# First MLP of a two-layer backbone: which of two engines splits the weights, and in what order output blocks are summed

## The chip, the cores and the metric

The kernel is one program on one core of a Trainium2 chip. The metric is device time in microseconds (us) of one execution. The kernel before took 1520.66 us (median of three runs, 1517.83 to 1520.87). The engines are named as the profile names them: PE is TensorE's matmuls and PEld its weight loads, DVE is VectorE, ACT ScalarE, POOL GpSimd, SP the queue of SyncE from which nearly all transfers start.

## The reference, cut to what matters

Two layers run over 512 latent tokens ("x") and a context of 256 ("c"), each of 1024 features. A layer normalises and modulates its tokens, projects them, mixes them in three parallel heads (windowed attention, gated chunks, a Fourier transform), projects back, and ends with an MLP:

```
def squared_relu_mlp(h, w1, w2):
    return jnp.square(jax.nn.relu(h @ w1)) @ w2      # w1 1024 x 4096, w2 4096 x 1024
...
    x = x + g1 * rmsnorm(y, g_post_mix[l])
    hx2 = rmsnorm(x, g_pre_ff[l]) * (1.0 + sc2) + sh2
    x = x + g2 * rmsnorm(squared_relu_mlp(hx2, w_ff1[l], w_ff2[l]), g_post_ff[l])
```

The scales and shifts come from a modulation, a product of a vector with a 1024 x 6144 weight for each layer. In the second layer the context ends after its keys and values, so its MLP has x alone; the first layer's MLP has x and c.

## The kernel before, in words

Every float32 operand of TensorE is kept as two parts, a high part (a rounded copy, made by ACT) and a low part (operand less high part), and each product is three: high by high, high by low, low by high. Making a low part is an elementwise instruction with two operands, which DVE or POOL can do.

The MLP runs over 16 groups of 256 hidden features. Groups 0 and 1 are plain products (`ff1_open`, `ff1`). From group 2 on the product with w1 is a Winograd form of Strassen's: `wino_open` loads two raw tiles of the group (L1133), makes eight weight operands "11", "21", "t1", "t2", "12", "t3", "t4", "22" (in that order) in `parts` (L1147 high part on ACT, L1148 low part) and the four differences between them in `sub` (L1152, which overwrite the raw tiles `raw_f`). `wino` then runs the products: tiles `w` and `wt` for x (L1182), `wc` for the context (L1195, `plain`). DVE adds them up (L1201, tiles `p`, `u`, `c`), and ACT makes the squared ReLU (`hidden`, L1122 to L1125) with tiles `hx` for x and `hc` for c. The features come in this order: first half of the tokens, first half of the group (`c11`); context, first half; second tokens, second half (`c22`); second tokens, first half (`c21`); first tokens, second half (the last sum, `u`, from the product `w22`); context, second half.

`ff2_open` loads two units of w2, 128 x 1024 each, and splits them (`wunit`: L234 high on ACT, L235 low, tile `lo_f`). `ff2` adds the group's products for one output block of 128 tokens (L1247, PSUM tiles `f2...`, three banks in turn) to its sum Y on DVE (L1251). In the first layer it goes over x2, x3, x0, x1, c0, c1, and after each block takes one step `ada` of the next modulation: a 512 KB load and two DVE multiply-adds of 128x1024 (L264, L266, tile `acc`).

What sets the order: each engine runs its own list in order. The program is scheduled when it is built: instructions go by the order of the code, as soon as the scheduler holds their inputs ready, and `high_priority(offset=...)` moves a part ahead by so many places; `HP` is that offset for `wino`. The table `LOADS` says, by layer, which engine takes each low part and difference: `lo1` and `diff1` begin anew with every group, `lo2` and `loh` run on through the layer. A `v` is DVE, a `p` POOL. In the first layer's mixing `MIX` says which steps of other work PE gets behind each attention unit (`flow`): `u`, `g`, `f` project one token block, `U`, `G`, `F` load their weights, `fc`, `fx` step through the Fourier part, `gc`, `gx` load a gate, `oc`, `ox` step through the output projection, `ada` through a modulation. Units are divided by `|`.

Of the kernel before, what the change touches and what calls it, by code (L numbers as in the profile page):

```python
# [18 lines left out]
P = 128  # L19
# [12 lines left out]
# How far the first product of the MLP goes ahead of other work.  # L32
HP = 5
# The engine (v or p) that takes each of the two-operand steps of a hidden group: low parts of the weights of the
# first and second product, differences of weights, low parts of the hidden features.
LOADS = {
    (0, 'lo1'): "vppvvppv",
    (0, 'diff1'): "vppv",
    (0, 'lo2'): "vp",
# [6 lines left out]
# What the tensor engine does beside the attention units of a layer: U, G, F load the weights of a column group  # L46
# of the in-projection and u, g, f project a token block with them, fc, fx step through the Fourier mixing,
# gc, gx load the gates, oc, ox step through the output projection, ada through a modulation.
MIX = (
    'U u u | u u u u G | ada ada g | ada g g ada ada g | g g ada | ada ada F f | f fc | f f f fc f fc | gc fx | gx oc fx oc oc | fx | ox ox ox ox oc',  # L50
    'U u u u G u g F g | | f f f f g | fx fx g fx | | | ox | ox ox ox gx',
# [10 lines left out]
def _bc(ap, n, axis):  # L62
    """ap with a broadcast dimension of n put in at free position `axis`."""
    v = ap.unsqueeze(axis)
    shape = list(v.shape)
    shape[axis] = n
    return v.to_broadcast(shape)
# [3 lines left out]
def kernel(ctx: ExitStack, tc: tile.TileContext, a: dict, out: bass.AP):  # L71
    nc = tc.nc
    PSUM = bass.MemoryType.PSUM
# [13 lines left out]
    # Temporaries of a chain come from h1, h2, h3 in this order, so that chains never wait in a circle.  # L87
# [9 lines left out]
    # Streams that run side by side have tiles of their own; within a tag tiles are handed out in program order.  # L97
# [25 lines left out]
    F = bank("F", 3)  # L123
# [9 lines left out]
    # ------------------------------------------------------------- constants  # L133
# [18 lines left out]
    def rows_in(name, width, pairs):  # L152
        """Rows at given partitions of a zeroed [32, width] tile."""
# [6 lines left out]
    def turned(t, name, use):  # L160
        """Feature-major pieces of four chunks of such rows in PSUM, handed to `use`."""
# [7 lines left out]
    # silu(c), silu(c_ctx) as two columns of a zero-padded stationary operand  # L169
# [18 lines left out]
    ones = unit[:, 1:2]  # L188
# [18 lines left out]
    # ---------------------------------------------------- common small helpers  # L207
# [4 lines left out]
    def power(o, i, scale, bias, expo):  # L212
        """o = (i * scale + bias) ** expo"""
# [11 lines left out]
    def wunit(src, shape, name, lo_eng=None, part=None, hi_pool=False):  # L225
        """A weight unit in two float32r parts whose sum is the float32 weight."""
# [11 lines left out]
    # ------------------------------------------------------------------ adaLN  # L238
    # modc[l]: feature-major columns for (sh1, sc1, sh2, sc2); gates go to DRAM rows.
# [7 lines left out]
    def ada_quad(l, q, alloc, alloct, wtile, side=None):  # L247
        """A sixth of the modulation of a layer. side: the rows of the weight times their entries are summed over
        the row chunks beside the tensor engine, which is left with the sum over the partitions."""
# [73 lines left out]
    def ada_rest(steps, alloc, alloct, side=None):  # L323
        """Steps through (layer, quad), one row chunk of the weight at a time."""
        for l, q in steps:
            yield from ada_quad(l, q, alloc, alloct, wa, side)
# [6 lines left out]
    # ------------------------------------------------- feature-major activations  # L333
    class Feat:
        """Feature-major tokens in two float32r parts, eight chunks of 128 features: with a tile for
        every chunk (whole=True, wide moving operands) or tiles for every token block."""
# [1077 lines left out]
```

## Time and profile before

| | us |
|---|---|
| median of three timed runs | 1520.66 (1517.83 to 1520.87) |
| span of the profiled execution | 1516.8 |
| PE busy | 1429.4 (94%) |
| DVE busy | 1115.8 (74%) |
| ACT busy | 747.7 (49%) |
| POOL busy | 644.3 (42%) |

Of the profiled execution the page gives the span, from its first to its last instruction; the median of the timed runs lies 3.9 us above it. Busy shares are means over unlike stages: the start (to about 106 us), mixing of the first layer (to 341), its MLP (to about 923), mixing of the second layer (to about 1140), its MLP. The page's list of costliest groups has both engines' instructions of the lines that the change touches, each with its idle time before it and what ended that idle time; a time in the queries counts from the span's start.

### The profile page before, as it was taken

The numbers are of one execution on the slowest core, as the hardware profiler recorded it, in microseconds if no ns is written. First come the engines' busy times: TensorE is split into PE (matmuls) and PEld (weight loads), VectorE is DVE, ScalarE is ACT, GpSimd is POOL, SyncE is SP. The second block draws the span as 40 slices with busy tenths as digits, with TensorE's granted clock in tenths as the row PEclk, the third lists the DMA queues.
The fourth block names the chain that finished last, engine by engine and source line by source line (L and its number), as shares of the span: only waits on it lengthen the run. The fifth ranks groups of instructions, "written<-read, shape, count | busy, mean of one in ns | idle before, by whom it ended". The sixth has DMA issues, their size and how long they took to land. (4 is left out here: it accounts for less than half of the span.)

```text
span 1516.8 us, 24509 instructions
## 1 busy us (share of the span) xinstructions
PE 1429.4 (94%) x9133; PEld 1252.7 (83%) x9133; DVE 1115.8 (74%) x2003; ACT 747.7 (49%) x1673; POOL 644.3 (42%) x608
## 2 busy tenths in 40 slices
PE   7999999999899999999989998999998899999997
PEld 4688798788788878888878887998777788989886
DVE  3366887858687877878777758788757987777685
ACT  3346666556534333343333445476656555554452
POOL 3212636646634333334433546234346644344241
PEclk9999999999999999999999999999998999999999
DMA  9634322435132332325554344213134133223322
GB/s 328 228 122 154 112 74 84 137 115 167 42 100 84 124 111 84 126 70 174 167 172 129 125 160 139 72 55 87 39 100 165 56 112 111 93 89 100 110 84 84
DMA packets 94352, 177.58 MB, mean 117 GB/s; under 512 B 5796, under 2 KB 59524, under 8 KB 94232
## 3 DMA queue, kind: packets, MB, share of 16 engines
q1 hardware_dynamic: 91224, 170.93, 35.0%
q0 software_dynamic: 3008, 5.08, 1.2%
q8 instruction: 72, 1.18, 0.3%
q14 instruction: 48, 0.39, 0.1%
HBM read 166.62 MB, written 9.46 MB: 116 GB/s over the span
## 5 line engine op out<-in xcount | busy, mean ns | idle before, releaser
L1152 POOL TENSOR_TENSOR raw_f<-raw_f,raw_f 128x512 f32<-128x512 f32 x70 | 98.2, 1402 | 107.8 <-DVE raw_f L1152 89.5
L1147 ACT CAST Wf<-raw_f 128x512 fp32r<-128x512 f32 x98 | 60.4, 619 | 118.6 <-DMA raw_f<-in_w_ff 108.4
L266 DVE SCALAR_TENSOR_TENSOR acc<-wa,silu,acc 128x1024 f32<-128x1024 f32 x70 | 96.1, 1391 | 21.7 <-DMA wa<-in_w_ada 21.6
L1148 POOL TENSOR_TENSOR Wf<-raw_f,Wf 128x512 fp32r<-128x512 f32 x28 | 40.1, 1433 | 153.3 <-ACT Wf L1147 153.3
L1195 PE MATMUL wc<-f01c,Wf 128*128 128x256 f32 x672 | 98.5, 286 | 3.4 <-DVE p L1201 3.4
L1195 PEld LDWEIGHTS wc<-f01c,Wf 128*128 128x128 f32 x672 | 91.6, 194 | 7.9 <-DVE p L1201 3.8
L1148 DVE TENSOR_TENSOR Wf<-raw_f,Wf 128x512 fp32r<-128x512 f32 x70 | 62.0, 887 | 41.0 <-ACT Wf L1147 40.9
L234 ACT CAST hi_f<-raw_f 128x1024 fp32r<-128x1024 f32 x72 | 73.8, 1043 | 34.8 <-PE f208c L1247 6.6
L235 POOL TENSOR_TENSOR lo_f<-raw_f,hi_f 128x1024 fp32r<-128x1024 f32 x20 | 54.7, 2735 | 77.7 <-ACT hi_f L234 57.6
L1125 DVE TENSOR_TENSOR hx<-r,hx 128x256 fp32r<-128x256 f32 x98 | 61.5, 630 | 31.2 <-ACT r L1124 31.1
L235 DVE TENSOR_TENSOR lo_f<-raw_f,hi_f 128x1024 fp32r<-128x1024 f32 x52 | 76.6, 1478 | 1.3 <-ACT hi_f L234 1.0
L1123 ACT ACTIVATE hx<-r 128x256 fp32r<-128x256 f32 x112 | 45.4, 413 | 44.4 <-PE f203x L1247 8.7
L1182 PE MATMUL w<-f11x,Wf 128*128 128x256 f32 x336 | 65.1, 283 | 0.0
L1182 PE MATMUL w<-S,Wf 128*128 128x256 f32 x336 | 63.0, 283 | 0.0
L1122 ACT ACTIVATE r<-c 128x256 f32<-128x256 f32 x84 | 34.7, 414 | 55.5 <-DVE c L1201 43.4
L1182 PEld LDWEIGHTS w<-f11x,Wf 128*128 128x128 f32 x336 | 54.7, 191 | 1.5
L1182 PEld LDWEIGHTS w<-S,Wf 128*128 128x128 f32 x336 | 53.0, 191 | 1.7 <-issue 0.4
L1182 PE MATMUL w<-f01x,Wf 128*128 128x256 f32 x336 | 50.4, 284 | 1.9 <-ACT Wf L1147 1.0
L1182 PEld LDWEIGHTS w<-f01x,Wf 128*128 128x128 f32 x336 | 46.4, 191 | 5.3 <-ACT Wf L1147 1.4
L1124 ACT ACTIVATE r<-r 128x256 f32<-128x256 f32 x112 | 45.5, 413 | 1.9
L393 ACT ACTIVATE xvx<-xTx,mod 128x256 f32<-128x256 f32 x64 | 31.6, 560 | 18.2 <-PE xTx L379 11.9
L797 ACT ACTIVATE E0x<-E0x,mx_0x 128x512 f32<-128x512 f32 (+1 forms) x32 | 24.9, 778 | 12.9 <-DVE mx_0x L791 12.7
(1243 smaller groups left out, 4886.1 us busy)
## 6 DMA issues: line engine op xcount, KB each, us to landing
raw_f<-in_w_ff SPq DMA_DIRECT2D x128, 512.0 KB
wa<-in_w_ada SPq DMA_DIRECT2D x80, 512.0 KB
wq<-in_w_ada SPq DMA_DIRECT2D x16, 512.0 KB
raw_out0c<-in_w_out SPq DMA_DIRECT2D x8, 512.0 KB
raw_out0x<-in_w_out SPq DMA_DIRECT2D x8, 512.0 KB
res0x<-xr0x SPq DMA_DIRECT2D x8, 512.0 KB
raw_out1x<-in_w_out SPq DMA_DIRECT2D x8, 512.0 KB
xl0x<-in_x SPq DMA_DIRECT2D x4, 512.0 KB
```

Of the source, the lines that this page charges most:

```text
L234: nc.scalar.copy(hi, raw)
L235: (lo_eng or nc.vector).tensor_tensor(out=lo, in0=raw, in1=hi.bitcast(F32), op=ALU.subtract)
L266: nc.vector.scalar_tensor_tensor(out=acc[r], in0=w, scalar=s, in1=acc[r], op0=ALU.mult, op1=ALU.add)
L1122: nc.scalar.activation(r, src, AF.Relu)
L1123: nc.scalar.activation(hv[:, 0], r, AF.Square)
L1124: nc.scalar.activation(r, r, AF.Square)
L1125: next(lo_h).tensor_tensor(out=hv[:, 1], in0=r, in1=hv[:, 0].bitcast(F32), op=ALU.subtract)
L1147: nc.scalar.copy(t[:, 0], src)
L1148: next(lo).tensor_tensor(out=t[:, 1], in0=src, in1=t[:, 0].bitcast(F32), op=ALU.subtract)
L1152: next(diff).tensor_tensor(out=o, in0=x, in1=y, op=ALU.subtract)
L1182: nc.tensor.matmul(ps, W[w][:, wl, k], A[k // 2][:, k % 2, xh], start=(m == 0), stop=(m == 11))
L1195: nc.tensor.matmul(ps, W[f"{k // 4 + 1}{j + 1}"][:, wl, k % 4], f2["c"].ap(k, xh, 0, CTX), start=(m == 0), stop=(m == 3 * KD - 1))
```

## The change

In the table of the first layer, `lo1` gives POOL three of eight low parts and not four ("21" goes to DVE), `diff1` one of four differences and not two (the one kept in tile b21, `raw_f`'s second), and `lo2` none of the low parts of w2 where it had every second one. Of a pattern of 16 letters for `lo1` only the first eight are used, since it begins anew with each group. The order of output blocks becomes x1, x2, x0, x3, c0, c1 in the first layer and x3, x0, x1, x2 in the second. `HP` goes from 5 to 4. In both layers some steps of the mixing move by a unit. Comment lines are gone as well.

```
-HP = 5
+HP = 4
 LOADS = {
-    (0, 'lo1'): "vppvvppv",
-    (0, 'diff1'): "vppv",
-    (0, 'lo2'): "vp",
+    (0, 'lo1'): "vvpvvppvvvpvvppv",
+    (0, 'diff1'): "vpvv",
+    (0, 'lo2'): "vv",
     (0, 'loh'): "vpvpvv",
...
 MIX = (
-    'U u u | u u u u G | ada ada g | ada g g ada ada g | g g ada | ada ada F f | f fc | f f f fc f fc | gc fx | gx oc fx oc oc | fx | ox ox ox ox oc',
-    'U u u u G u g F g | | f f f f g | fx fx g fx | | | ox | ox ox ox gx',
+    'U u u | u u u u G | ada ada g | ada g g ada ada ada g | g | ada g ada F f | f fc | f f f fc f fc | fx gc | gx oc fx oc oc | fx | ox ox ox ox oc',
+    'U u u u G u g F g | f | f f g | f fx fx g fx |  |  | ox | ox ox ox gx',
 )
...
+        order = ((("x", 1), ("x", 2), ("x", 0), ("x", 3), ("c", 0), ("c", 1)),
+                 (("x", 3), ("x", 0), ("x", 1), ("x", 2)))[l]
         for g in range(2, NG):
...
-                for kd, b in [(kd, b) for kd, b in (("x", 2), ("x", 3), ("x", 0), ("x", 1), ("c", 0), ("c", 1)) if kd in kinds]:
+                for kd, b in order:
                     ff2([g], kd, b)
                     next(ada, None)
```

In the order below, names carry layer, group and part: `Wf106t3` is operand t3 of layer 0, group 6, `raw_f1060` the first raw tile of w1 of that group, `lo_f2061` the low part of its second unit of w2, `hx060` and `hx061` the first and second half of its features. POOL's list for group 6 of the first layer, before:

```order
L1148 TENSOR_TENSOR Wf10621_6229<-raw_f1061_6221,Wf10621_6229 128x512
L1148 TENSOR_TENSOR Wf106t1_6233<-raw_f1060_6219,Wf106t1_6233 128x512
L1152 TENSOR_TENSOR raw_f1060_6219<-raw_f1061_6221,raw_f1060_6219 128x4x128
L1152 TENSOR_TENSOR raw_f1061_6221<-raw_f1061_6221,raw_f1060_6219 128x4x128
L1125 TENSOR_TENSOR hx050_5885<-r0521_6045,hx050_5885 128x256
L235 TENSOR_TENSOR lo_f2051_6108<-raw_f2051_6105,hi_f2051_6107 128x1024
L1125 TENSOR_TENSOR hc05_5884<-r05c0_5975,hc05_5884 128x256
L1148 TENSOR_TENSOR Wf106t3_6245<-raw_f1060_6219,Wf106t3_6245 128x512
L1148 TENSOR_TENSOR Wf106t4_6248<-raw_f1061_6221,Wf106t4_6248 128x512
L235 TENSOR_TENSOR lo_f2061_6447<-raw_f2061_6444,hi_f2061_6446 128x1024
L1125 TENSOR_TENSOR hc06_6223<-r06c0_6314,hc06_6223 128x256
L1125 TENSOR_TENSOR hx060_6224<-r0621_6384,hx060_6224 128x256
```

and now:

```order
L1148 TENSOR_TENSOR Wf106t1_6233<-raw_f1060_6219,Wf106t1_6233 128x512
L1152 TENSOR_TENSOR raw_f1060_6219<-raw_f1061_6221,raw_f1060_6219 128x4x128
L1125 TENSOR_TENSOR hx050_5885<-r0521_6045,hx050_5885 128x256
L1125 TENSOR_TENSOR hc05_5884<-r05c0_5975,hc05_5884 128x256
L1148 TENSOR_TENSOR Wf106t3_6245<-raw_f1060_6219,Wf106t3_6245 128x512
L1148 TENSOR_TENSOR Wf106t4_6248<-raw_f1061_6221,Wf106t4_6248 128x512
L1125 TENSOR_TENSOR hc06_6223<-r06c0_6314,hc06_6223 128x256
L1125 TENSOR_TENSOR hx060_6224<-r0621_6384,hx060_6224 128x256
```

Operand 21, the second difference and the low part of w2 are gone from POOL, in this group as in the others; in all its list has 565 rows where it had 609. DVE's list around the low parts of that group's w2, before:

```order
L1251 TENSOR_TENSOR Y0c1_4441<-Y0c1_4441,f205c11_6210 128x512
L1201 TENSOR_TENSOR p106_6254<-p106_6254,wt206_6332 128x256
L235 TENSOR_TENSOR lo_f2060_6441<-raw_f2060_6438,hi_f2060_6440 128x1024
L1201 TENSOR_TENSOR u406_6346<-p106_6254,wt106_6319 128x256
L1201 TENSOR_TENSOR c2206_6361<-u406_6346,wt306_6348 128x256
L1201 TENSOR_TENSOR p106_6254<-p106_6254,wt306_6348 128x256
L1201 TENSOR_TENSOR c2106_6382<-p106_6254,wt406_6369 128x256
L1125 TENSOR_TENSOR hx061_6225<-r0622_6363,hx061_6225 128x256
```

and now:

```order
L1251 TENSOR_TENSOR Y0c1_4441<-Y0c1_4441,f205c11_6210 128x512
L1201 TENSOR_TENSOR c2106_6382<-p106_6254,wt406_6369 128x256
L235 TENSOR_TENSOR lo_f2060_6441<-raw_f2060_6438,hi_f2060_6440 128x1024
L1201 TENSOR_TENSOR u406_6346<-u406_6346,w2206_6389 128x256
L235 TENSOR_TENSOR lo_f2061_6447<-raw_f2061_6444,hi_f2061_6446 128x1024
L264 TENSOR_SCALAR acc110_6518<-wa110_6520,silu_84 128x1024
L1125 TENSOR_TENSOR hx061_6225<-r0612_6403,hx061_6225 128x256
L283 COPY arow10_6511<-ada10_6502 128x256
L264 TENSOR_SCALAR acc111_6519<-wa110_6520,silu_84 128x1024
```

Both low parts of w2 now stand on DVE, one ahead of the last sum `u406`, one behind it and ahead of the low part of `hx061` that this sum leads to. PE's list in group 10 from the last product `w22` on (`wc1010`, `wc0011` are products of the context, `w11011`, `w21011` of the next group), before, where the first output block needs the features `hx0100` of the second tokens, whose product ended 15 matmuls ahead of these rows:

```order
L1182 MATMUL w22010_7788<-S040_4688,Wf101022_7650 128x256 x6
L1182 MATMUL w22010_7788<-S041_4695,Wf101022_7650 128x256 x6
L1195 MATMUL wc1010_7807<-f01c2_3211,Wf101022_7650 128x256 x3
L1195 MATMUL wc1010_7807<-f01c3_3212,Wf101022_7650 128x256 x6
L272 MATMUL ada12_7903<-acc120_7519,unit_107 32x256 x4
L1247 MATMUL f2010x20_7849<-hi_f20100_7839,hx0100_7623 128x512
L1247 MATMUL f2010x20_7849<-lo_f20100_7840,hx0100_7623 128x512
L1247 MATMUL f2010x21_7857<-hi_f20100_7839,hx0100_7623 128x512
L1247 MATMUL f2010x21_7857<-lo_f20100_7840,hx0100_7623 128x512
```

and now, where block x1, begun earlier with the first half of its features, ends with `hx0101`, which come from the last product; ahead of these rows stand, in this order, the last six matmuls of `w22010`, four of `ada12`, two of `w11011` and one of `f2010x20`:

```order
L1247 MATMUL f2010x20_7868<-lo_f20100_7840,hx0100_7623 128x512
L1195 MATMUL wc0011_8066<-f01c0_3209,Wf101111_8003 128x256 x2
L1182 MATMUL w21011_8046<-f01x02_3847,Wf101121_8006 128x256 x2
L1247 MATMUL f2010x20_7868<-hi_f20100_7839,hx0100_7623 128x512
L1247 MATMUL f2010x20_7868<-hi_f20101_7845,hx0101_7624 128x512
L1247 MATMUL f2010x20_7868<-lo_f20101_7846,hx0101_7624 128x512
L1247 MATMUL f2010x20_7868<-hi_f20101_7845,hx0101_7624 128x512
L1182 MATMUL w11011_8032<-f01x00_3845,Wf101111_8003 128x256 x4
L1182 MATMUL w11011_8032<-f01x01_3846,Wf101111_8003 128x256 x6
L1195 MATMUL wc0011_8066<-f01c0_3209,Wf101111_8003 128x256 x4
L1195 MATMUL wc0011_8066<-f01c1_3210,Wf101111_8003 128x256 x3
L1247 MATMUL f2010x10_7849<-hi_f20101_7845,hx0101_7624 128x512
```

Block x2 now stands among the next group's products, and the first use of `hx0101` for block x1 is the last row. SP's list of transfers is the same but for neighbours that change places.

## Rows read from the trace of the kernel before

**Rows 1.** Busy time in stretches: us, engines' busy (instructions), PE clock, DMA share, GB/s.

```profile
core 0: us, PE busy (x) PEld busy (x) DVE busy (x) ACT busy (x) POOL busy (x), PEclk, DMA share, GB/s
106.00:341.00 235.00, 226.90 (x1492) 194.95 (x1492) 176.23 (x459) 147.38 (x365) 117.05 (x149) 1.00 0.36 113
...
396.00:440.00 44.00, 35.83 (x203) 31.36 (x202) 43.35 (x46) 15.86 (x30) 21.83 (x14) 0.92 0.27 84
440.00:865.00 425.00, 405.24 (x2521) 357.56 (x2520) 328.07 (x451) 162.58 (x352) 169.95 (x118) 1.00 0.39 123
...
923.00:1140.00 217.00, 204.92 (x1379) 185.26 (x1379) 162.57 (x408) 131.04 (x310) 87.88 (x108) 0.98 0.25 78
...
1200.00:1400.00 200.00, 200.00 (x1239) 180.38 (x1239) 158.40 (x254) 100.83 (x208) 84.13 (x60) 1.00 0.32 101
```

**Rows 2.** PE's waits from 440 to 865: total us, times, longest.

```profile
PE wc L1195 <- DVE p L1201: 3.4, 2, 2.8
PE f205x L1247 <- DVE lo_f L235: 2.3, 1, 2.3
PE f206x L1247 <- DVE Y0x L1251: 1.9, 1, 1.9
PE f204x L1247 <- DVE Y0x L1251: 1.7, 2, 1.0
PE ada L272 <- DVE p L1201: 1.7, 1, 1.7
PE f2013x L1247 <- DVE Y0x L1251: 1.4, 1, 1.4
...
PE w L1182 <- ACT r L1122: 0.8, 1, 0.8
...
PE f208x L1247 <- POOL hx L1125: 0.7, 1, 0.7
...
PE f2011x L1247 <- ACT hx L1123: 0.6, 1, 0.6
```

**Rows 3.** Timeline at 550: start, us, engine and instruction, [idle before].

```profile
550.30 2.39 POOL L235 TENSOR_TENSOR lo_f<-raw_f,hi_f 128x1024 fp32r<-128x1024 f32 x1 [0.97 <-ACT hi_f L234]
550.39 2.85 DVE L1152 TENSOR_TENSOR raw_f<-raw_f,raw_f 128x512 f32<-128x512 f32 x1
...
553.16 1.74 DVE L235 TENSOR_TENSOR lo_f<-raw_f,hi_f 128x1024 fp32r<-128x1024 f32 x1
...
554.96 0.50 PE L1247 MATMUL f205x<-lo_f,hx 128*128 128x512 f32 x1 [2.27 <-DVE lo_f L235]
```

**Rows 4.** Tile raw_f from 440 to 865: ns min/median/max of its DVE instructions.

```profile
L1148 DVE TENSOR_TENSOR Wf<-raw_f,Wf x36: 678/692/2878, 444.6 to 847.3; 128x512 fp32r<-128x512 f32 x36
...
L235 DVE TENSOR_TENSOR lo_f<-raw_f,hi_f x13: 1212/1226/2836, 449.9 to 863.9; 128x1024 fp32r<-128x1024 f32 x13
...
L1152 DVE TENSOR_TENSOR raw_f<-raw_f,raw_f x12: 676/680/2847, 445.8 to 842.0; 128x512 f32<-128x512 f32 x12
```

**Rows 5.** Groups on POOL from 440 to 865: xcount | busy us, mean ns | idle before.

```profile
L1152 POOL TENSOR_TENSOR raw_f<-raw_f,raw_f 128x512 f32<-128x512 f32 x26 | 37.3, 1436 | 1.5
L235 POOL TENSOR_TENSOR lo_f<-raw_f,hi_f 128x1024 fp32r<-128x1024 f32 x13 | 35.7, 2748 | 75.3 <-ACT hi_f L234 55.2 <-PE wt L1182 20.1
L1148 POOL TENSOR_TENSOR Wf<-raw_f,Wf 128x512 fp32r<-128x512 f32 x13 | 17.5, 1344 | 101.6 <-ACT Wf L1147 101.6
```

**Rows 6.** Timeline of DVE and PE at 788.

```profile
788.45 1.21 DVE L235 TENSOR_TENSOR lo_f<-raw_f,hi_f 128x1024 fp32r<-128x1024 f32 x1
789.59 1.27 DVE L266 SCALAR_TENSOR_TENSOR acc<-wa,silu,acc 128x1024 f32<-128x1024 f32 x1
790.78 0.41 DVE L1201 TENSOR_TENSOR p<-p,wt 128x256 f32<-128x256 f32 x1
...
791.25 0.98 PE L1195 MATMUL wc<-f01c,Wf 128*128 128x256 f32 x6 [2.81 <-DVE p L1201]
```

**Rows 7.** Timeline at 720, group 10: last product, its sum, its features.

```profile
719.54 1.60 PE L1182 MATMUL w<-S,Wf 128*128 128x256 f32 x12
...
724.48 0.41 DVE L1201 TENSOR_TENSOR u<-u,w 128x256 f32<-128x256 f32 x1
...
725.51 0.41 ACT L1123 ACTIVATE hx<-r 128x256 fp32r<-128x256 f32 x1
```

## The prediction

> **What bounds the kernel now.** I read the busy time by stretches first, then PE's waits in the stretch that the change touches most, then the timeline ahead of each of those waits, and last the groups of instructions on POOL and the durations on DVE.
>
> By stretches the reader is to see where PE has anything to give back [rows 1]. In the second layer's MLP PE is busy 200.00 of 200 us: nothing there waits, so the second layer's new block order, which moves no work, can gain nothing and can lose only by a wait it makes. In the steady part of the first layer's MLP (440 to 865) PE is busy 405.2 of 425, so 19.8 us are idle, at a full clock (1.00, the 2.4 GHz level). In the start of the Winograd groups (396 to 440) it is idle 8.2 of 44 us and the clock averages 0.92; DVE is busy 43.35 of 44 there. The two mixing stretches leave 8.1 and 12.1 us.
>
> PE's waits in the steady part [rows 2] nearly all end with DVE: with its adds (p, Y) that free a PSUM bank, or with a low part (lo_f). Yet DVE is busy only 328 of 425 us [rows 1]. So it isn't short of time; it is late at certain moments. One such moment shows why [rows 3]: at 550.39 a difference that normally takes 0.68 us takes 2.85, because at 550.30 POOL had begun the low part of a w2 unit, 2.39 us long, and both read two operands from SBUF. The next DVE instruction, lo_f, ends late, and PE sits idle 2.27 us for it. The durations on DVE say the same [rows 4]: medians of 0.69, 1.23 and 0.68 us lie at the minima, maxima at 2.88, 2.84 and 2.85. The median instruction is not held; some are held for up to 2.2 us by a POOL instruction that came first.
>
> **The change part by part.** The first layer has 14 Winograd groups and 16 groups in all. POOL loses 14 low parts "21", 14 differences and 16 low parts of w2. At their means in the steady part [rows 5] that is 14 x (1.34 + 1.44) + 16 x 2.75 = 83 us of POOL. DVE gains the same 44 instructions at its unheld medians [rows 4]: 14 x (0.69 + 0.68) + 16 x 1.23 = 39 us. In the steady part there are 13 of each: POOL drops 72 of its 170 us, DVE gains 34 on 328.
>
> Relief. I took each wait of rows 2 and asked in the timeline whether a DVE instruction ahead of it was held by, or a POOL one queued behind, one of those that move. It was so, wholly, for f205x (2.3), ada behind p (1.7), f2013x (1.4), w behind r (0.8) and f208x behind POOL's own hx (0.7, queued behind a low part of w2); for the first of f204x's two (0.7), half of f206x (0.9, the other half behind the difference that stays on POOL), and 0.6 of wc's longest. Sum 9.1 us: the upper end. The lower end lets the moved instruction stand at the same place on DVE and take its own time there: three at 1.2 and three at 0.7 come back, 5.7, which leaves 3.4. The order shows the low parts of w2 on DVE after the adds of the wt products in group 6, not among the preparation of weights where they held it, so I take 6.
>
> Added DVE work. 34 us go into 97 us of idle DVE time, so most of it is hidden; the cover is gone where DVE is already in a row of work that PE waits for, as at 788 [rows 6], where a low part (1.21) and a multiply-add (1.27) stand ahead of p and PE waits 2.81. Bounds: 0, and 1.2 us in each of 12 groups, 14.4. 34 us on 328 is a tenth, and a tenth of the some 10 us of waits that relief doesn't explain is 1. I take +1, near the lower end, since the schedule was made anew with these instructions in it.
>
> Block order in the first layer. The first block to finish is now x1 and not x2. x1 needs the features from the last product. In group 10 [rows 7] that product ended at 721.14, its sum at 724.89, its high features at 725.92: 4.8 us. In the new order of that group 23 matmuls of 256 columns and 6 of 512 lie between; at 1.60 / 12 = 0.13 us for the former (same rows) and twice that for the latter, 4.6 us. Before, x2 had an equally short way from its own product: 36 matmuls of 256 columns, 4.8 us, and some waits of this kind are in rows 2 (f2011x behind ACT's hx 0.6, f208x behind POOL's 0.7). What x2 waited for was in part a low part made on POOL; x1's last one is made on DVE. I count 0, between -1.3 (both of those waits go) and +10, the rival below.
>
> Start of the groups (396 to 440). One more operand and one more difference ahead of DVE's S chain cost 1.4 us where DVE is full, and the second low part 1.2; in return POOL's three, 5.5 us of the 21.8 there, no longer hold it. 0, between -2 and +3. The clock's 0.92 falls on short stretches at half speed behind idle PE; if those waits go, 1.7 us come back, which I don't count.
>
> Mixing. The moved steps issue the same instructions. One modulation step (a load and four matmuls) goes one unit earlier past a projection, one gating projection one unit later, a Fourier step changes place with the gate load, and in the second layer one Fourier projection goes a unit earlier and one a unit later; SP's queue only sees neighbours exchanged. With 8.1 and 12.1 us of idle there [rows 1] I count 0, within 4 either way. The second layer's MLP and HP: 0, up to +2 if the new order makes a first wait.
>
> Sum: -6 + 1 = -5 on the span of 1516.8, so 1511.8. The timed median lies 3.9 above the profiled span; carried over, that is 1515.7.
>
> **The rivals.** *DVE becomes the bound* (slower). Both low parts of w2 stand back to back with a multiply-add ahead of the low part of hx061, as the order of group 6 shows (there with an accumulator's first multiply), and PE needs that one for x1. If each of 12 steady groups pays 1.2 us for the second low part, it costs 14.4 against 6 of relief: +8.4, 1529. It wins from 5 groups on that pay. For it: DVE has only 97 us of idle left and 63 after. Against: its median instruction isn't late, only held ones are. The Trainium skill, Perfetto Trace Analysis, Optimizing Scalar/DVE Operations, speaks for it: it says that moving work between GpSimd and DVE might not help since they share a read port, and that with DVE saturated one would offload from it. Its condition, a saturated DVE, the trace shows only from 396 to 440.
>
> *x1 comes too late* (slower, the same sign by another place). If four of the groups between 440 and 865 get their last features 2.5 us past their first use, about what one hold of 2.2 us [rows 4] adds to the 0.2 us by which group 10 would be late, PE waits 10 us more: with the sum above +5, 1525. Against it: before, these features weren't wanted early, and both ACT and DVE did other work first.
>
> *One hold for another* (no change). The moved instructions read two operands on DVE too, so POOL's remaining ones wait for them, and its hx and hc come late instead. The relief falls to its lower end, 3.4, and added work takes 2 to 3: 1520. The Trainium skill, SBUF — State Buffer, Who interferes with whom, states it: a DVE instruction with two SBUF inputs and a GpSimd one that reads SBUF hold each other off, and the order of issue decides which is blocked. The trace agrees on DVE's side (2.85 for 0.68). By this rule alone the time would be that 1520.
>
> *The whole tail goes* (faster still). DVE's lateness falls together, the wait at 788 and the start's 8 us included, and with them the stretches at half clock: relief 9, another 3 in the start and 2 of clock, less 1: -13, 1508.
>
> **How the numbers follow.** The forecast has 0.40, the larger gain 0.12, no change 0.22, the two slower ones 0.17 and 0.09. A measurement of this kernel tells 0.2%, 3 us, from no change. So faster is 0.52, within 0.2% 0.22, slower 0.26. The likeliest case alone runs from 1511 to 1518. The range holds all but about 2 in 10: from 1505, inside the larger gain, to 1529, the price of the slower rival.
>
> **What would show it.** Right: in the steady part POOL near 100 us; DVE near 345 to 360, its longest weight instruction under 2 us; PE's waits there down from 19.8 to about 15, with those behind lo_f gone. Wrong: waits of f2 products for x1 behind hx or u in most groups, or DVE over 375 with PE's waits behind Y and p longer. A change of more than 3 us in the second layer's MLP or the mixing would say that another edit decides.

## The result, and the profile after

The changed kernel takes 1502.33 us (median of four runs, 1499.84 to 1505.52) beside 1519.83 for the kernel before on the same chip: a ratio of 0.9892, 95% interval 0.9876 to 0.9907. A later set of runs gave 1503.87 beside 1516.86, 0.9919 (0.9901 to 0.9938). The profiled span fell from 1516.8 to 1500.2 us. Faster, as forecast, but by 17.5 us (13.0 in the later set) and not 5, and 2.7 us below the low end of the range. Of all timed runs below one, of mix1_only, is slow (1574.01 us at a granted clock of 0.845) and stands in no median or ratio.

Busy time by stretches in the profile after, columns as in [rows 1]:

```profile
core 0: us, PE busy (x) PEld busy (x) DVE busy (x) ACT busy (x) POOL busy (x), PEclk, DMA share, GB/s
395.00:435.00 40.00, 32.48 (x190) 28.30 (x189) 40.00 (x45) 13.86 (x26) 17.92 (x11) 0.96 0.29 92
435.00:853.00 418.00, 407.06 (x2529) 359.70 (x2528) 330.54 (x491) 163.34 (x355) 101.44 (x79) 0.99 0.40 125
911.00:1125.00 214.00, 203.09 (x1380) 184.76 (x1380) 160.00 (x409) 130.23 (x310) 87.31 (x108) 0.98 0.24 78
1185.00:1386.00 201.00, 200.38 (x1244) 180.62 (x1244) 161.67 (x256) 100.07 (x208) 84.91 (x60) 1.00 0.31 100
```

In the steady part PE is now idle 10.9 us (418 less 407.06) and no longer 19.8 (of 425). POOL is down from 170 to 101 us. DVE took over 40 instructions there (491 for 451) and is still busy only 330.5 us, since the others shrank. PE's waits of that stretch, total us, times, longest:

```profile
PE w L1182 <- ACT Wf L1147: 8.1, 5, 3.3
PE f205x L1247 <- DVE Y0x L1251: 1.4, 1, 1.4
PE f2013x L1247 <- DVE lo_f L235: 0.6, 1, 0.6
PE ada L272 <- DVE c L1201: 0.4, 1, 0.4
PE f209x L1247 <- DVE Y0x L1251: 0.3, 1, 0.3
```

Against [rows 2] the waits that end with DVE are all but gone. The wait in their place is for the next group's first high part on ACT, in groups 10 to 14. Durations of DVE's weight instructions, ns min/median/max, against [rows 4]:

```profile
L1148 DVE TENSOR_TENSOR Wf<-raw_f,Wf x49: 675/685/1544, 436.2 to 843.1; 128x512 fp32r<-128x512 f32 x49
L1152 DVE TENSOR_TENSOR raw_f<-raw_f,raw_f x25: 679/687/1231, 439.5 to 849.9; 128x512 f32<-128x512 f32 x25
L235 DVE TENSOR_TENSOR lo_f<-raw_f,hi_f x25: 1214/1221/2080, 444.3 to 851.7; 128x1024 fp32r<-128x1024 f32 x25
```

Medians are the same, the maxima fell from 2.85 to 1.2, 1.5 and 2.1 us. On POOL the costliest group of [rows 5] is halved in number, the low parts of w2 are gone:

```profile
L1152 POOL TENSOR_TENSOR raw_f<-raw_f,raw_f 128x512 f32<-128x512 f32 x13 | 18.3, 1408 | 1.0
```

The new wait at its longest, in the timeline of SP's queue, ACT and PE (start, us, [idle before]):

```profile
729.20 13.84 SPq L252 DMA_DIRECT2D wa<-in_w_ada  x6
744.91 2.44 SPq L1133 DMA_DIRECT2D raw_f<-in_w_ff  x2
...
749.40 0.62 ACT L1147 CAST Wf<-raw_f 128x512 fp32r<-128x512 f32 x1 [2.24 <-DMA raw_f<-in_w_ff]
...
753.12 1.22 PE L1182 MATMUL w<-f01x,Wf 128*128 128x256 f32 x4 [3.33 <-ACT Wf L1147]
```

Six loads of the modulation stand ahead of w1's on SP's queue and share its four buffers; ACT waits for the transfer and PE for ACT.

### The profile page after: what moved, and what is told of

Read it like the earlier page. It is cut to its first block, busy times and chain, and to the rows that moved or that the text cites. A ratio compares the mean times of both kernels' runs of the same rounds, so it can differ in the third digit from the quotient of the medians.

```text
span 1500.2 us, 24535 instructions
## 1 busy us (share of the span) xinstructions
PE 1421.0 (95%) x9133; PEld 1248.2 (83%) x9133; DVE 1116.8 (74%) x2047; ACT 746.4 (50%) x1673; POOL 562.3 (37%) x564
## 5 line engine op out<-in xcount | busy, mean ns | idle before, releaser
L1152 POOL TENSOR_TENSOR raw_f<-raw_f,raw_f 128x512 f32<-128x512 f32 x56 | 77.1, 1377 | 111.4 <-DVE raw_f L1152 89.5
L266 DVE SCALAR_TENSOR_TENSOR acc<-wa,silu,acc 128x1024 f32<-128x1024 f32 x70 | 88.6, 1282 | 23.0 <-DMA wa<-in_w_ada 23.0
L235 DVE TENSOR_TENSOR lo_f<-raw_f,hi_f 128x1024 fp32r<-128x1024 f32 x68 | 96.6, 1431 | 5.5 <-ACT hi_f L234 5.5
L1195 PE MATMUL wc<-f01c,Wf 128*128 128x256 f32 x672 | 94.6, 283 | 0.0
L1148 DVE TENSOR_TENSOR Wf<-raw_f,Wf 128x512 fp32r<-128x512 f32 x84 | 66.6, 796 | 36.0 <-ACT Wf L1147 35.6
L1125 DVE TENSOR_TENSOR hx<-r,hx 128x256 fp32r<-128x256 f32 x98 | 53.9, 559 | 19.2 <-ACT r L1124 19.1
L1182 PEld LDWEIGHTS w<-f01x,Wf 128*128 128x128 f32 x336 | 49.2, 203 | 12.7 <-ACT Wf L1147 10.1
L1148 POOL TENSOR_TENSOR Wf<-raw_f,Wf 128x512 fp32r<-128x512 f32 x14 | 19.7, 1405 | 43.0 <-ACT Wf L1147 43.0
L1125 POOL TENSOR_TENSOR hx<-r,hx 128x256 fp32r<-128x256 f32 x14 | 13.0, 927 | 57.8 <-ACT r L1124 57.8
```

The costliest lines, as they stand in the source:

```text
L235: (lo_eng or nc.vector).tensor_tensor(out=lo, in0=raw, in1=hi.bitcast(F32), op=ALU.subtract)
L266: nc.vector.scalar_tensor_tensor(out=acc[r], in0=w, scalar=s, in1=acc[r], op0=ALU.mult, op1=ALU.add)
L1125: next(lo_h).tensor_tensor(out=hv[:, 1], in0=r, in1=hv[:, 0].bitcast(F32), op=ALU.subtract)
L1148: next(lo).tensor_tensor(out=t[:, 1], in0=src, in1=t[:, 0].bitcast(F32), op=ALU.subtract)
L1152: next(diff).tensor_tensor(out=o, in0=x, in1=y, op=ALU.subtract)
L1182: nc.tensor.matmul(ps, W[w][:, wl, k], A[k // 2][:, k % 2, xh], start=(m == 0), stop=(m == 11))
```

## Experiments

Theory A: POOL's reading of operands holds DVE, and the held instructions are what PE waits for. B: the new block order is the gain. C: it is chance, since every edit shuffles the lists. D: only waiting for POOL's own slow results ended. The table has every run on the full kernel. MLP is the time from the first Winograd matmul to the last matmul of group 13's output blocks, "mixing" from there to the last matmul of tile h100x in the second layer, "tail" from the last matmul of tile f218x (output blocks of the second layer's group 8) to PE's last; the 188 to 191 us between these two are left out. "Stretch" sums, over DVE's instructions of the MLP, each one's time above the shortest of its line and shape. DVE busy counts once where the records of two instructions overlap. All in us, worked out from each run's trace; the ratio is of timed runs to the kernel before on the same chip. The expectations speak of the stretch of the steady part alone: worked out in the same way, it is 50.0 before, 26.8 in loads_only, 23.2 in the changed kernel and 5.0 in a_nopool.

| run | ratio (interval) | start | MLP | mixing | tail | DVE busy in MLP | stretch |
|---|---|---|---|---|---|---|---|
| before | 1 | 399.9 | 463.4 | 312.1 | 144.0 | 365.8 | 61.7 |
| before_again | one run | 402.2 | 464.3 | 312.8 | 141.9 | 365.1 | 60.9 |
| changed | 0.9892 (0.9876–0.9907) | 398.2 | 452.6 | 310.1 | 141.9 | 365.2 | 31.7 |
| after_again | 0.9919 (0.9901–0.9938) | 397.3 | 453.6 | 310.2 | 141.3 | 366.8 | 33.5 |
| loads_only | 0.9951 (0.9935–0.9967) | 399.7 | 458.0 | 313.7 | 140.0 | 367.2 | 35.7 |
| blk0_only | 0.9996 (0.9984–1.0008) | 402.5 | 462.4 | 314.6 | 141.4 | 363.2 | 59.2 |
| loads_blk0 | 0.9950 (0.9935–0.9964) | 400.7 | 453.5 | 313.7 | 140.0 | 366.3 | 32.7 |
| mix1_only | 0.9986 (0.9974–0.9998) | 401.5 | 462.8 | 311.5 | 143.8 | 365.6 | 61.2 |
| a_noloads | 0.9985 (0.9974–0.9996) | 399.5 | 461.0 | 312.1 | 141.1 | 362.5 | 58.3 |
| a_mixold | 0.9948 (0.9931–0.9964) | 399.0 | 453.3 | 312.6 | 140.9 | 368.3 | 36.0 |
| a_pooltt | 1.0124 (1.0103–1.0145) | 403.2 | 481.3 | 313.5 | 140.9 | 404.2 | 71.6 |
| a_poolset | 1.0002 (0.9990–1.0014) | 402.0 | 467.4 | 311.8 | 141.1 | 372.0 | 35.9 |
| a_bal | 0.9895 (0.9875–0.9916) | 399.5 | 451.5 | 312.9 | 141.3 | 370.0 | 39.0 |
| a_g2 | 0.9944 (0.9927–0.9961) | 399.1 | 456.0 | 311.8 | 141.7 | 370.2 | 34.9 |
| a_nopool | 0.9879 (0.9862–0.9895) | 401.8 | 447.6 | 307.7 | 141.0 | 385.3 | 11.4 |
| b_nopool | 0.9883 (0.9867–0.9898) | 400.0 | 447.6 | 310.2 | 140.4 | 383.7 | 11.8 |
| a_allv | 0.9848 (0.9835–0.9861) | 402.9 | 448.5 | 306.9 | 135.8 | 385.6 | 11.8 |
| b_allv | 0.9874 (0.9855–0.9892) | 400.2 | 447.3 | 310.5 | 135.8 | 383.8 | 12.6 |
| allv_early | 0.9802 (0.9785–0.9819) | 401.8 | 438.5 | 309.6 | 135.8 | 383.5 | 12.3 |

### The shares alone, and all but the shares

loads_only (on the kernel before; a_noloads is the changed kernel with these lines turned back):

```
-    (0, 'lo1'): "vppvvppv",  (0, 'diff1'): "vppv",  (0, 'lo2'): "vp",
+    (0, 'lo1'): "vvpvvppv",  (0, 'diff1'): "vpvv",  (0, 'lo2'): "vv",
```

> The kernel before with the new table of shares alone. Theory A, DVE held by POOL: the 15 us of matmul waits that ended with DVE in the steady groups go with this table, so it gives 9 to 14 of the 17.5 us, 1506 to 1511 us, and DVE's instructions there stretch by some 25 us in sum and no longer 50. Theory B, the block order lets products of the next group run while the last features are made: the table gives 2 to 6 us, 1514 to 1518 us. Theory C, any edit shuffles PE's list and the gain is chance: no forecast, but then a_noloads need not give back what this one gains.

> The changed kernel with the old table of shares, everything else new. A: what the table gave is lost, 1512 to 1517 us, and the waits that end with DVE or with POOL's lo_f are back (over 10 us in the steady groups). B: 1503 to 1507 us.

Measured 1511.12 (6 runs) and 1516.10 (12). loads_only gave 7.4 us by its ratio, less than A's 9 to 14 and more than B's 2 to 6; a_noloads fell where A put it, with 15.1 us of waits behind DVE. Each set taken alone, the shares are the greater part: 0.5% with them, 0.15% with all the rest, and A's stretch goes with them: 35.7 with the new table, 58 to 62 with the old. But the parts don't add up to the 0.8 to 1.1% of the whole. What the new shares leave in PE's waits from 435 to 853:

```profile
PE w L1182 <- DVE c L1201: 3.0, 3, 1.4
PE w L1182 <- ACT Wf L1147: 2.8, 2, 1.5
PE ada L272 <- DVE c L1201: 2.0, 1, 2.0
PE f2012x L1247 <- DVE Y0x L1251: 1.6, 1, 1.6
```

In all 10.6 us still end with DVE, mostly with c and Y0x, where the changed kernel has 2.7 and the kernel before 15.7 (from 440 to 865). They are of another kind, though. I took each wait of 0.2 us or more and summed, over the unbroken row of up to six DVE instructions ahead of it, the time above the shortest of their line and shape. Before, that covers 9.0 of 15.5 us; with the new shares 1.2 of 10.3; in the changed kernel 0.6 of 2.7. So the waits behind held instructions go with the shares, and those behind a DVE that is late without being held rise from 6.5 to 9.1.

### The block order alone, and with the shares

```
-  for kd, b in [... (("x", 2), ("x", 3), ("x", 0), ("x", 1), ("c", 0), ("c", 1)) ...]:
+  for kd, b in ((("x", 1), ("x", 2), ("x", 0), ("x", 3), ("c", 0), ("c", 1)), (second layer as before))[l]:
```

> The kernel before with the first layer's new block order alone. If the order is the other part of the steady gain (2 us in the kernel without the new shares): 1 to 3 us less in the steady groups, 1514.5 to 1517 us. Theory B in its strong form, the order is the gain: 1505 to 1510 us. My forecast's value for it was no change, its bounds -1.3 to +10 us.

> The kernel before with the new shares and the first layer's new block order together, nothing else. Alone they gave 7.4 us and nothing. If the two work on each other (with the shares DVE's results come sooner, and the order gives PE products to run in what waits are left): 11 to 15 us less than before, and the steady groups 6 to 8 us shorter as in the changed kernel. If they add up: 6 to 8 us less, the steady groups 4 to 5 us shorter.

Alone: 1518.63 beside 1518.88, no change, MLP 1.0 us shorter. B falls. With the shares the MLP is 453.5, 9.9 us shorter where the two alone give 5.4 and 1.0: they work on each other by 3.5 us. Its waits in the same stretch begin so:

```profile
PE w L1182 <- ACT Wf L1147: 7.8, 4, 2.6
PE wt L1182 <- ACT r03c L1122: 0.8, 1, 0.8
PE f205x L1247 <- DVE Y0x L1251: 0.8, 1, 0.8
```

The waits for c and Y0x went (1.9 us in all end with DVE). The span is 1506.0 us, 3.7 below that of loads_only, but the profile is of the fastest of its five runs and that of loads_only of the third slowest of six. The timed ratio is that of loads_only, where I had expected 11 to 15 us: the intervals leave some 3 us between the two. So that shares and order work on each other is seen in the trace and not in the timed runs.

### The mixing steps

mix1_only puts the second layer's new line of MIX into the kernel before; a_mixold puts both old lines into the changed one.

> The kernel before with the second layer's new mixing steps alone. If they are what shortened that stage by 2.5 us (the changed kernel and the one without the new shares both show it, the one with the shares alone does not): 2 to 3 us less between 923 and 1175 us, nothing before it, 1514 to 1516.5 us. If that gain is chance: within 1 us of before in that stage.

> The changed kernel with the old mixing steps in both layers. If the new steps have a part in the gain of their own: 2 to 5 us above the changed kernel, and the second layer's mixing about 2 us longer. If where a stage's small waits fall is chance (the second layer's steps alone gave 1 us in that stage): within 2 us of the changed kernel.

Measured 1517.13 beside 1518.88, and 1508.44 beside 1516.06. That stage: 0.6 us less with the new steps, 2.5 more with the old. Over all profiles it lies between 306.9 and 313.5 with the new steps (eleven) and 310.2 and 314.6 with the old (eight). The means are 310.7 and 312.5: the steps are worth some 2 us here, less than the scatter. In time a_mixold stands 0.3 to 0.6% above the changed kernel's two sets; its span is only 2.9 us above, but the profiled execution was the fastest of its six, 3.5 us below their median.

### What holds DVE: the disputed cost by itself

micro computes nothing of the model; its code in short:

```
sections of: for i in range(24): vector.tensor_tensor(v[:, :512], va, vb)      # DVE, from SBUF
beside:      for i in range(12): gpsimd.tensor_tensor(g[:, :512], ga, gb)      # or fills, or one operand, or nothing
```

> None of the model is computed: twelve stretches in which DVE repeats one instruction, alone or with POOL repeating one beside it, with no data between the two. Theory A, POOL's reading of two SBUF operands holds DVE: DVE's 128x512 difference takes 0.68 us alone and 1.3 us or more in the mean beside POOL's differences, 0.68 us beside POOL's fills; DVE's add with one operand in PSUM stays at 0.68 us beside POOL's differences. The multiply-add of 128x1024 goes from 1.2 us towards 2. Rival D, DVE waits only for results of POOL: no stretch beside anything.

DVE's groups (names: DVE's instruction, then POOL's beside it; mean ns of one behind the busy time), then POOL's:

```profile
L87 DVE TENSOR_TENSOR v3two_two<-va,vb 128x512 f32<-128x512 f32 x24 | 28.7, 1197 | 1.3 <-ACT va L125 0.6
L87 DVE TENSOR_TENSOR v2two_two<-va,vb 128x512 f32<-128x512 f32 x24 | 27.9, 1162 | 17.5 <-ACT va L125 16.7
...
L93 DVE SCALAR_TENSOR_TENSOR v8mac_two<-va,vb 128x1024 f32<-128x1024 f32 x12 | 25.1, 2088 | 0.9 <-ACT va L125 0.5
L90 DVE TENSOR_SCALAR v7one_two<-va 128x1024 f32<-128x1024 f32 x16 | 22.4, 1398 | 1.1 <-ACT va L125 0.5
L87 DVE TENSOR_TENSOR v5two_one<-va,vb 128x512 f32<-128x512 f32 x24 | 22.3, 930 | 1.4 <-ACT va L125 0.6
L87 DVE TENSOR_TENSOR v4two_set<-va,vb 128x512 f32<-128x512 f32 x24 | 16.6, 692 | 1.3 <-ACT va L125 0.5
L87 DVE TENSOR_TENSOR v0two__71<-va,vb 128x512 f32<-128x512 f32 x24 | 16.6, 692 | 6.2 <-DMA vb<-in_x 5.4
L98 DVE TENSOR_TENSOR v6psum_two<-va,pa 128x512 f32<-128x512 f32 x24 | 16.5, 688 | 13.0 <-ACT va L125 12.2
```

```profile
L87 POOL TENSOR_TENSOR g2two_two<-ga,gb 128x512 f32<-128x512 f32 x12 | 19.1, 1595 | 1.3 <-ACT ga L126 0.4
...
L87 POOL TENSOR_TENSOR g_two<-ga,gb 128x512 f32<-128x512 f32 x12 | 15.1, 1262 | 23.7 <-ACT ga L126 22.8
```

DVE's difference takes 0.692 us alone (v0) and beside POOL's fills (v4), 1.162 beside POOL's differences (v2); its add from PSUM isn't touched (v6). No data passes between the two, so D is out as the only reason. The 1.162 falls short of the 1.3 expected, since POOL's twelve were done after 19.1 of DVE's 27.9 us; the multiply-add went to 2.088 us, as expected. In the kernel before, from 440 to 865, the same is seen: 63 of DVE's 451 instructions ran 0.15 us or more past the shortest of their line and shape, and every one of them overlapped a two-operand instruction of POOL; together they have 46.8 of the 50.0 us of stretch. The price: 24 instructions took 27.9 us in place of 16.6, so each of POOL's twelve differences cost a DVE that never rests 0.94 us, where DVE makes one itself in 0.69; each of the six of 128x1024 (v3) cost (28.7 - 16.6) / 6 = 2.0 us, where DVE makes one in 1.22 [rows 4]. The Trainium skill, SBUF — State Buffer, Who interferes with whom, says that a DVE instruction with two SBUF inputs contends with a GpSimd one that reads SBUF and not with one that only writes; the rows agree on both.

### More work on POOL

a_pooltt, on the changed kernel, three such calls (shortened here) in each group of the first layer (behind "21", behind "t2", and of twice the size behind w2); a_poolset fills dum in their place:

```
+  gpsimd.tensor_tensor(out=dum[:, :512], in0=<a high part made on ACT>, in1=bd, op=subtract)
```

> The changed kernel, and in each group of the first layer POOL makes four more differences of 128x512 from two SBUF operands into a spare tile that nobody reads: about the work that the change took from it (5.5 us a group). A: the stretch of DVE's instructions in the steady groups rises from 23 to 40 us or more, and the time by 6 to 13 us, to 1508 to 1515 us, though no one waits for the added results. Rival D, the gain came from no longer waiting for POOL's own slow results: within 2 us of the changed kernel.

> As a_pooltt, but POOL fills the spare tile with a constant for about as long (5.9 us a group, by 0.94 and 0.53 us for fills of 128x1024 and 128x512) and reads nothing. A, if it is the reading of operands that holds DVE: stretch stays near 23 us, time within 3 us of the changed kernel, 1500 to 1505 us. If any work of POOL slows DVE or the kernel: as a_pooltt, 1508 to 1515 us.

a_pooltt took 1538.84 us, more than twice the cost expected: the MLP is 28.7 us longer than the changed kernel's, DVE's stretch 71.6. One place in its timeline:

```profile
628.20 1.12 DVE L1160 TENSOR_TENSOR raw_f<-raw_f 128x512 f32<-128x512 f32 x1
...
628.74 1.74 POOL L1124 TENSOR_TENSOR dum<-hi_f,bd 128x512 f32<-128x512 f32 x1
...
629.25 2.31 DVE L235 TENSOR_TENSOR lo_f<-raw_f,hi_f 128x1024 fp32r<-128x1024 f32 x1
...
631.48 1.21 DVE L1156 TENSOR_TENSOR Wf<-raw_f,Wf 128x512 fp32r<-128x512 f32 x1
...
632.10 1.72 POOL L1124 TENSOR_TENSOR dum<-Wf,bd 128x512 f32<-128x512 f32 x1
632.61 0.41 DVE L1211 TENSOR_TENSOR c<-p,wt 128x256 f32<-128x256 f32 x1
...
633.16 1.19 PE L1192 MATMUL w<-f01x,Wf 128*128 128x256 f32 x4 [2.74 <-DVE c L1211]
```

Three instructions ahead of c took 4.6 us where their unheld times sum to 2.6, and PE waited 2.74 us for c, though nobody reads dum. The added ones also stand ahead of POOL's own work in its queue; the two effects aren't parted here. a_poolset is inconclusive: the fills wait for no data, so they were put ahead, into the first layer's mixing, where POOL has 171 us in 226 instructions:

```profile
105.00:340.00 235.00, 223.51 (x1478) 191.87 (x1468) 173.46 (x454) 142.79 (x354) 171.19 (x226) 0.99 0.34 107
```

(148 instructions and 117 us in the changed kernel.) So its 1518.91 us are no test of A; what fills do beside DVE, micro tells. Its MLP, with none of the fills in it and a stretch of 35.9, is still 14.8 us longer than the changed kernel's; why stays open.

### No work on POOL

a_nopool and b_nopool, on the changed kernel and the kernel before; a_allv and b_allv do the same in the second layer too:

```
+    (0, 'lo1'): "vvvvvvvv",  (0, 'diff1'): "vvvv",  (0, 'lo2'): "vv",  (0, 'loh'): "vvvvvv",
+    (1, 'lo1'): "vvvvvvv",   (1, 'diff1'): "vvvv",                       # a_allv, b_allv
```

> The changed kernel with all low parts and differences of the first MLP on DVE, none on POOL. Theory A in its strong form, the holding is all that costs: the stretch falls from 24 us to under 5, and the time by 2 to 5 us more. If DVE's own time is then the bound (some 80 instructions of 0.41 to 0.69 us more, about 50 us, for 24 us of stretch less: DVE busy over 90% of a group): 1505 to 1520 us, slower than the changed kernel.

> The kernel before with all low parts and differences of the first MLP on DVE, in the old block order. If shares and order work on each other: 8 to 12 us less than before, the steady groups 8 to 10 us shorter, where the new order has 15.8. If they add up: the steady groups 14 to 15 us shorter.

> The changed kernel with all low parts and differences of both MLPs on DVE. If the holds are still what costs after the change: 3 to 8 us below the changed kernel beside it, steady groups of the first layer 4 to 5 us shorter as when the first layer alone was so, and DVE busy 85% there. If that was chance: within 2 us. The second layer, where PE is busy to 99.7%, gives 0 to 2 us, in its tail.

> The kernel before with all low parts and differences of both MLPs on DVE, all else as before. If the shares are the whole matter: 21 to 25 us less than before, as a_allv, which has all of the change beside it (23.2 us less). If the other parts of the change are worth their own: 16 to 20 us less.

Measured 1497.98, 1498.59, 1493.66 and 1498.38. What A's strong form foretold came (a stretch of 5.0 in the steady part, 2 to 6 us less time by the ratios), and the bound by DVE is not reached: in the MLP of a_nopool DVE is busy 385.3 of 447.6 us, 86% for 81% in the changed kernel, and the MLP is 5 us shorter. The steady part of a_allv:

```profile
435.00:853.00 418.00, 408.97 (x2569) 360.17 (x2568) 355.10 (x575) 167.52 (x362) 4.50 (x6) 1.00 0.40 126
```

84 more instructions on DVE than after, 24.6 us more busy. b_nopool reaches the same 447.6 us in the old order: where nothing holds DVE, the order is worth nothing; that is 15.8 us less than before, where I expected 8 to 10 if shares and order work on each other, 14 to 15 if they add up. In the second layer all v gives 5 us in the tail (135.8 for 141). a_allv is 10.2 us below the changed kernel beside it. b_allv gains 19.3 us, which lies in the range for the other parts being worth their own (16 to 20) and not in that for the shares alone (21 to 25). Its ratio is 0.0026, some 4 us, above that of a_allv, and the intervals overlap. The spans, 1493.1 and 1493.2, don't decide it: they are of the fastest of five runs of b_allv and the slowest of five of a_allv. So in the MLP no part of the change but the shares is seen to matter then (447.3 and 448.5); whether the others give up to 4 us outside it stays open.

### The modulation's steps, and the new wait

a_bal takes seven steps in groups 2 to 8 and five in 9 to 13, a_g2 none in group 2 and seven in 3 to 10; allv_early is a_allv with w1's loads moved:

```
                 for i, (kd, b) in enumerate(order):
                     ff2([g], kd, b)
+                    if i == 3 and not last and g < NG - 3:
+                        RAW[g + 1] = w1_load(g + 1)
                     next(ada, None)
```

> The changed kernel with the modulation's steps spread otherwise over the first MLP: seven in groups 2 to 8, five in groups 9 to 13, and no longer six in each, since the later steps load 512 KB each and the earlier ones every second time. If the new waits for ACT's first high part (8.1 us in groups 10 to 14) come from w1's transfers queued behind six such loads: they go, with the half-clock stretches after them, 1493 to 1499 us. If DVE, with one more multiply-add of 1.2 us in seven groups, becomes the bound there: 1501 to 1507 us.

> The changed kernel, but group 2 takes no steps of the modulation and groups 3 to 10 take seven. At the start of the Winograd groups DVE is busy without a gap from 394 to 435 us, 7.6 us of it six multiply-adds of the modulation, and two matmul waits end with it there (3.2 us for lo_f of w2, 3.5 us for the sum Y0c). If DVE's queue is the cause: the second wait goes, 2 to 5 us less than the changed kernel. If the added steps in eight groups cost as much: within 2 us of it.

> a_allv, and the two loads of the next group's w1 are issued after a group's fourth block, ahead of the last two steps of the modulation and no longer behind them. If that queue makes the wait: the waits for ACT's first high part (some 7 us in groups 8 to 13) fall under 3 us and the time to 3 to 7 us below a_allv, a ratio of 0.980 to 0.983. If the loads of w2, which then come into the ring's slots of w1, are late instead: waits for hi_f or lo_f in their place, and a ratio of 0.984 or more.

a_bal 1503.78 and a_g2 1508.99: misses, no gain and a loss. In a_bal the waits for Wf nearly went (0.6 us left), but others (hx, hi_f, Y0) came. allv_early took 1487.41 us, as expected of it, 0.9802 of the kernel before. Its steady part and its longest waits:

```profile
435.00:853.00 418.00, 414.38 (x2637) 368.79 (x2636) 359.64 (x582) 171.81 (x369) 10.23 (x6) 1.00 0.42 132
```

```profile
PE f2012c L1253 <- DVE Y0x L1257: 1.1, 1, 1.1
PE f2013x L1253 <- ACT hi_f L234: 0.9, 1, 0.9
PE f2012x L1253 <- DVE Y0x L1257: 0.7, 1, 0.7
```

PE is idle 3.6 of 418 us (the last 12.7 of them lie behind its MLP, which ends at 840.3); the waits for ACT's first high part, 5.9 us in a_allv, are gone. It is the fastest version: by the ratios to the kernel before, 7 us below a_allv and 14 to 18 below the changed kernel.

### The same programs again

> The kernel before, unchanged, profiled once more. If the tail's 5.8 us of waits for the sums Y1x (against 1.8 us with the same lists of the second layer behind the new shares) are a matter of one execution: another amount here, the tail 2 to 3 us shorter. If they follow from where the program enters that stage: 5 to 6 us again. The stages ahead of it within 1 us but for the half-clock stretches.

> The changed kernel, unchanged, timed and profiled once more beside the next two. Stages within 1 us of the first profile if they are fixed by the lists; the start and the second layer's mixing up to 2.5 us longer if a half-clock stretch there comes and goes from one execution to the next.

The MLP and the mixing come back within 1 us. The start differs by 2.3 and 0.9 us, the tail of the kernel before by 2.1 (141.9 for 144.0): its waits for the sums Y1x were in part those of one execution. loads_only and loads_blk0, whose lists there are those of the kernel before, have 140.0.

## Why the prediction was right and wrong

**What bounds it, and the relief: right.** DVE late at single moments, in the larger part held by POOL, was the cause. For relief less added work the sum had -5; the shares alone made the MLP 5.4 us shorter. That the two agree so well is in part luck, since both terms were too small by about 2: the waits behind held instructions fell by 7.8 us (9.0 to 1.2), not 6, and those behind a DVE that is late by its own list rose by 2.6 (6.5 to 9.1), not 1. POOL near 100 us came (101.4), the waits behind lo_f are gone but for 0.6. DVE came out at 330, not 345 to 360, since the stretch fell with the moved work, and its longest weight instruction at 2.08, not under 2.

**The step that failed: "Block order in the first layer ... I count 0".** Worked out alone it was right (blk0_only: 0.9996). Beside the new shares the traces give it 4.5 us of MLP (458.0 to 453.5), outside its bounds of -1.3 to +10: the waits for c and Y0x that the shares leave, nearly all behind a DVE that isn't held, are gone. I added terms priced one at a time. Taken the other way round, the order gives 1.0 and the shares beside it 8.9 (462.4 to 453.5), where the sum has 5; to which of the two terms the 3.5 us between belong the runs can't say, only that the sum of the two left them out. The order is worth nothing again once POOL makes none of these parts. The timed runs of loads_only and loads_blk0 don't tell the two apart, so its share of the time stays open. That PE has products of the next group to run in those moments is argued from the lists, not shown. The working behind the 0 also left out the four matmuls of `ada12` that stand between the last product and the first use of its features.

**Terms counted at nothing.** The 13.4 us between 1515.7 and 1502.3 are: MLP 5.8 (10.8 shorter, -5 forecast), start 1.6, mixing 2.0, tail 2.1, 0.1 in the second layer's MLP, and 1.8 because the median lies 2.1 us and not 3.9 above the profiled span. PE's idle time fell in the MLP (27.9 to 18.5 us) and by 1.5 us in the tail, and nowhere else. In the start it rose from 23.3 to 25.3, and the same 2535 matmuls were busy 372.9 us for 376.5, at a granted clock of 1.00 for 0.99; a_allv, with the same new steps, has 378.1 at 0.98. In the mixing PE is idle 18.4 for 18.0, busy 291.7 for 294.1. Start and tail differ by as much between two executions of the kernel before, so nothing shows that they are the edit's. Of the mixing, within its 4 either way, the new steps may have the whole; the timed runs give them 4 to 8 us behind shares and order (a_mixold against the changed kernel's sets), more than any stage of the trace shows, and that stays open too.

**The rivals.** *DVE becomes the bound*: refuted for the MLP as a whole; even at 86% busy it is shorter. *x1 comes too late*: no such wait in the profile after. *One hold for another*, and the rule of the Trainium skill (SBUF — State Buffer, Who interferes with whom) by which it would come out at 1520: holding is mutual (POOL's difference goes from 1.26 to 1.60 us in micro), but the stretch fell by half with POOL's instructions. *The whole tail goes*, 1508, was the nearest, and still too small; that by its number alone, for the start of the groups, on which it counted, still has PE idle 7.5 of 40 us (8.2 of 44 before) behind a DVE that is busy all the time. (The clock it wanted back there was mis-sized as well: the profile before has two stretches of 3.4 and 3.5 us at 0.50, so about 3.4 us and not 1.7.)

**The new wait** for w1's transfers, 8.1 us, stood in no part of the prediction. SP's order hadn't changed; the wait grew as DVE's lateness went (1.0 us before, 2.8 in loads_only, 7.8 in loads_blk0).

HP and the first layer's mixing steps weren't tried alone.

## What to carry to other kernels

Price POOL's two-operand work not only by its own time but by what it takes from a busy DVE: here 0.94 us for a part that DVE makes in 0.69. Where PE waits for DVE and DVE is held, try giving DVE the work back, here all of it, and look at once for the wait that lay behind. Don't add prices of edits that act on the same wait; try them together.

## What the hardware showed unexpectedly

DVE's one-operand multiply of 128x1024 from SBUF, 0.694 us alone, takes 1.398 beside POOL's differences (v7). Alone:

```profile
L90 DVE TENSOR_SCALAR v10one__404<-va 128x1024 f32<-128x1024 f32 x16 | 11.1, 694 | 0.8 <-ACT va L125 0.3
```

The Trainium skill, SBUF — State Buffer, Who interferes with whom, exempts an instruction with one SBUF input only outside the modes in which DVE takes the second port pair, and lists this kind among those that can enter them; the rows fit, but show no mode. A one-operand instruction on POOL (v5) holds DVE too: 0.930 for 0.692. DVE busy 86% of a 448 us stretch did not slow PE.
